# Split products for the first two weights of well-filled experts, branches on three engines, gate and scatter one group later

## The chip, the cores and the metric

The kernel runs on one core of one Trainium2 chip. The metric is the device time of one execution in microseconds (us). PE is the tensor engine, ACT the scalar engine (ScalarE), DVE the vector engine (VectorE), POOL is GpSimd, and SP issues the DMAs.

## The reference

The program is a decoder trunk of two layers over 256 tokens of width 1024. Each layer has a mixer (attention, convolution, a state-space part), a feed-forward part and a gated embedding. In the second layer the feed-forward part is a sum over eight experts of inner width 3584, of which each token uses its best two:

```python
def swiglu(x, w1, w3, w2):
    return (jax.nn.silu(x @ w1) * (x @ w3)) @ w2

def moe_swiglu(x, router, w1, w3, w2):
    logits = (x @ router).astype(jnp.float32)
    top_vals, top_idx = lax.top_k(logits, TOP_K)
    wts = jax.nn.softmax(top_vals, axis=-1)
    comb = jnp.einsum('blk,blke->ble', wts, jax.nn.one_hot(top_idx, N_EXPERTS, dtype=jnp.float32))
    for e in range(N_EXPERTS):
        y = y + comb[..., e:e + 1] * swiglu(x, w1[e], w3[e], w2[e])
```

All weights are f32, 44 MB an expert.

## The kernel before

**Loads.** `moe` goes through the experts one behind the other. `expert_loads` cuts an expert's weights into 42 loads of 1 MB (128 partitions by 2048 f32). The inner width is taken in four chunks (`CHUNKS`): three of 1024 columns, one of 512. A full chunk has four loads of w1 and four of w3, the last chunk two and two; 14 loads of w2 follow. `load` takes the next slot of a ring of 1 MB buffers (`self.ring`, `room`) and has SP issue the DMA. In the second layer the ring has 18 slots, built in `run`: buffers of earlier stages that are free by then, among them the four split buffers (`hl`) and one buffer of the residual stream (`xl`). A slot is written again when the products that read it are done. At the seventh expert (`e == OVF`) two slots go to the overflow path, which this input does not take, and the other 16 are all loaded ahead.

**Products.** `expert` emits groups of two loads (`GRP`) inside `either`, which is a branch on the expert's number of tokens `n`: over 64 (`SM`), plain f32 products with 128 columns of tokens as the weights of PE; up to 64, the two halves of a chunk run as products of 64 columns in two halves of PE. Both write the two accumulators `mgu` of w1, then of w3 (L1468); w2 writes `mo` (L1503). Only PE reads `n` and branches; the other engines have only unconditional jumps between the blocks. An expert's w1 and w3 make 14 groups, w2 seven. A plain f32 product shows in the trace as two records.

**Gate, turn, scatter.** Behind the last w3 group of a chunk ACT applies Silu to w1's accumulators (L1475) and DVE multiplies with w3's (L1476), half by half. What is put into the list `todo` is emitted behind the next group by `flush`: `turn`, which has PE transpose the gated values (`hT`, L1444) and ACT and DVE copy them into `ht` (L1449, L1447), and for the finished expert `scatter`, which multiplies its result with the slot matrix on PE and adds it to `y` on DVE (L1526). The result is first split into a high and a low part (`ot`, L313 on ACT and L314 on DVE). DVE also clears accumulators (L1432).

**Split products.** Elsewhere (the dense feed-forward, the last gate) a weight is split into `whl`: ACT copies it to the reduced-precision type f32r (L313), DVE subtracts that from the weight (L314), 1024 columns at a time in `parts`; `mm3` (L308 to L310) then makes three products: high by high, low tokens by high weight, high tokens by low weight.

A scheduler sets the order within each engine; each engine takes its instructions strictly in that order.

Of the kernel before, what the change touches and what calls it, by code (L numbers as in the profile page):

```python
# [7 lines left out]
F32 = mybir.dt.float32  # L8
F32R = mybir.dt.float32r
I32 = mybir.dt.int32  # L10
U32 = mybir.dt.uint32
AF = mybir.ActivationFunctionType
# [3 lines left out]
P = 128  # L16
D = 1024
S = 256
TT = S // P
KT = D // P  # L20
# [135 lines left out]
RBN = 2  # L156
OV = 2
HB = 4
GRP = 2
SM = 64  # L160
OVF = 6
# [31 lines left out]
class Trunk:  # L193
# [1042 lines left out]
    def moe(self, l, mp):  # L1236
        nc, a, sm = self.nc, self.a, self.sm
# [100 lines left out]
        for e in range(NE):  # L1338
            if e == OVF:

                self.flush()
                ov = self.over
                main = self.turned(ov[:2])
                self.ring, self.nload = main, 0
                self.pre = [self.load(*s) for s in self.expert_loads(j, e)[: len(main)]]
                self.ring, self.nload = [ov] * ov[2], 0
                pre, self.pre = self.pre, []
                self.overflow(j, mp, Da[:, e // 2 % 2], cint, th, tl, rank, sel, comb, y)
                self.ring, self.pre, self.nload = main + self.ring, pre, len(main)
                pair(e)  # L1350
            Dm = Da[:, e // 2 % 2]
            es = ts(e % 2)
            De = [Dm[:, tt, e % 2] for tt in range(TT)]
            D2 = mp.tile([P, TT, P], F32, tag="D2", name="D2")
            for tt in range(TT):
                nc.vector.tensor_scalar(D2[:, tt], slots, rank2[:, tt, e : e + 1], sel[:, tt, e : e + 1], op0=ALU.is_equal, op1=ALU.mult)
            ce = [comb[:, tt, e : e + 1] for tt in range(TT)]
            n = nc.tensor.value_load(cint[0:1, e + 1 : e + 2], min_val=0, max_val=S)
            ahead = (lambda: pair(e + 1)) if e % 2 and e + 1 not in (OVF, NE) else None
            last = e == NE - 1  # L1360
            self.expert(mp, self.expert_loads(j, e), n, self.xh[:, :, es], De, [D2[:, tt] for tt in range(TT)], ce, y, ahead, norm if last else None)
            if e == NE - 2:

                lnp = self.ln_params(l, 1, mp, "tl")
                more = mp.tile([P, 2, D], F32R, tag="th", name="more")
                bias = self.ple_bias(l, mp.tile([P, D], F32, tag="h2", name="gb"), more[:, 0])
# [34 lines left out]
                    yield  # L1401

    def flush(self):
        while self.todo:
            self.todo.pop(0)()

    def either(self, n, emit):

# [9 lines left out]
    def expert(self, mp, loads, n, xe, Dm, D2, comb, y, ahead=None, done=None):  # L1418

        nc = self.nc
        mm = nc.tensor.matmul
        loads = iter(loads)
        get = lambda: [self.pre.pop(0) if (s := next(loads)) and self.pre else self.load(*s) for _ in range(GRP)]
        rows = (slice(0, SM), slice(P - SM, P))

        def pair(name):
            acc = self.pair(name)
            if n is not None:  # L1430
                for h in range(2):
                    nc.vector.memset(acc[h][rows[1 - h]], 0.0)  # L1432
            return acc

        hts = []

        def turn(ci, hw, hbs):

            nb = hw // P
            ht = mp.tile([P, 2 * nb, P], F32, tag=f"h{ci}", name="ht", bufs=1)  # L1440
            for h in range(2):
                ps = self.tr("hT")
                for i in range(nb):
                    nc.tensor.transpose(ps[:, i * P : (i + 1) * P], hbs[h][:, i * P : (i + 1) * P], self.ident)  # L1444
                dst = ht[:, h * nb : (h + 1) * nb].rearrange("p k t -> p (k t)")
                if h:
                    nc.vector.tensor_copy(dst, ps[:, :hw])  # L1447
                else:
                    nc.scalar.activation(dst, ps[:, :hw], AF.Copy)  # L1449
                hts.extend((ht[:, h * nb + i], h) for i in range(nb))  # L1450

        DT = []
        for ci, (c0, cw) in enumerate(CHUNKS):
            hw, ku = cw // 2, 2048 // cw
            accs = []
            for wi in range(2):
                acc = pair("mgu")
                for u0 in range(0, KT // ku, GRP):
                    ws = get()

                    def emit(few):
                        for u, w in enumerate(ws):
                            for i in range(ku):
                                k = (u0 + u) * ku + i
                                for h in range(2):
                                    wk = w[:, i, h * hw : (h + 1) * hw]
                                    dst, x = (acc[h][rows[h], :hw], xe[:, k, 0:SM]) if few else (acc[h][:, :hw], xe[:, k])
                                    mm(dst, x, wk, start=k == 0, stop=k == KT - 1)  # L1468

                    self.either(n, emit)  # L1470
                accs.append(acc)
            hbs = []
            for h in range(2):
                hb = mp.tile([P, 512], F32, tag="hb", name="hb", bufs=2)
                nc.scalar.activation(hb[:, :hw], accs[0][h][:, :hw], AF.Silu)  # L1475
                nc.vector.tensor_mul(hb[:, :hw], hb[:, :hw], accs[1][h][:, :hw])  # L1476
                hbs.append(hb)
            self.todo.append(lambda ci=ci, hw=hw, hbs=hbs: turn(ci, hw, hbs))
            if ci == 0:

                def turn_slots():

                    t = mp.tile([P, 2, TT, P], F32R, tag="DT", name="DT", bufs=1)
                    ps = self.tr("DT")
                    for i, src in enumerate([v.bitcast(F32) for v in Dm] + D2):
                        nc.tensor.transpose(ps[:, i * P : (i + 1) * P], src, self.ident)
                    nc.scalar.activation(t.rearrange("p h t s -> p (h t s)"), ps, AF.Copy)
                    DT.append(t)

                self.todo.append(turn_slots)  # L1490
        acc = pair("mo")
        NK = D_FFE // P
        for g in range(0, NK // 2, GRP):
            ws = get()

            def emit(few):
                for u, w in enumerate(ws):
                    for i in range(2):
                        k = 2 * (g + u) + i
                        ht, hf = hts[k]  # L1500
                        for h in range(2):
                            dst, x = (acc[h][rows[h]], ht[:, rows[hf]]) if few else (acc[h], ht)
                            mm(dst, x, w[:, i, h * 512 : (h + 1) * 512], start=k == 0, stop=k == NK - 1)  # L1503

            self.either(n, emit)
            if g == GRP and ahead:
                ahead()
        ots = []
        for h in range(2):
            ot = mp.tile([P, 2, 512], F32R, tag=f"h{h}", name="ot", bufs=1)  # L1510
            self.split(ot[:, 0], ot[:, 1], acc[h])
            ots.append(ot)

        def scatter():
            normed = ()
            if done:
                self.ring, self.nload = self.turned((self.cp, "xl")), 0
                self.new_xT()
            for tt in range(TT):
                sc = self.pair("sc")  # L1520
                for h in range(2):
                    hs = slice(h * 512, (h + 1) * 512)
                    mm(sc[h], DT[0][:, h, tt], ots[h][:, 0], start=True, stop=False)
                    mm(sc[h], DT[0][:, h, tt], ots[h][:, 1], start=False, stop=True)
                    with self.after(*normed):
                        nc.vector.scalar_tensor_tensor(y[:, tt, hs], sc[h], comb[tt], y[:, tt, hs], op0=ALU.mult, op1=ALU.add)  # L1526
                if done:
                    normed = done(tt)[1:]

        if n is None or done:  # L1530
            scatter()
        else:
            self.todo.append(scatter)

    def overflow(self, j, mp, Dm, cint, th, tl, rank, sel, comb, y):

# [91 lines left out]
    def rest(self, l, ffn):  # L1628
        pool = lambda n: self.tc.tile_pool(name=f"{n}{l}", bufs=1)

        with self.open, pool("ra") as ra, pool("re") as re, pool("rd") as rd, pool("rb") as rb, pool("th") as th:
            if l % 2:
                self.ring = [(rb, "raw", RBN)] * RBN + [(self.st, "raw", RB)] * RB + [(self.xp, "pp", 1), (ra, "raw", 1)]
                self.ring += [(self.st, "hl", HB)] * HB + [(self.cp, "xl", 1)]
                self.ring += [(re, "raw", 2)] * 2
                self.nload = len(self.ring) - 2
                self.over = (rd, "raw", OV)
                self.ring += [self.over] * OV
# [52 lines left out]
```

## Time and profile before

| what | value |
|---|---|
| median of 3 runs | 1608.57 us (1608.24 to 1608.64) |
| the profiled execution, its own time | 1610.99 us |
| its span in the profile | 1608.8 us |
| mean granted clock of PE | 0.959 |
| PE busy | 1454.2 us, 90% of the span |
| DVE, ACT busy | 678.0 us (42%), 401.3 us (25%) |
| 16 DMA engines, q1 | 73.3% of the span, 437.42 MB |
| expert loads | 336 of 1024 KB |

The expert stage lies between about 620 and 1536 us of the span. A busy share is a mean over stages with different limits; the chain of waits (what ended last, followed back) and windows of single stretches tell which of them sets the time. Inside a bracket behind a row of a timeline stands the idle time of that engine just before the row and what ended it.

### The profile page before, as it was taken

How to read it: one execution, taken by the hardware profiler on the slowest of the kernel's cores; microseconds unless marked ns; L12 is line 12 of the kernel's file. 1: busy time of each engine (PE TensorE's matmuls, PEld its weight loads, DVE VectorE, ACT ScalarE, POOL GpSimd, SP SyncE). 2: the span in 40 equal slices, each digit the busy share in tenths (PEclk: the TensorE clock that was granted, in tenths of full speed). 3: DMA queues.
4: the chain of work that ended last, by engine and by line, in shares of the span. 5: the costliest groups of instructions: out<-in, count | busy, mean ns of one | idle time of the engine just before them, and what ended most of it. 6: DMA issues, size and time to landing. Idle time of an engine off the chain costs nothing. (4 is left out here: it accounts for less than half of the span.)

```text
span 1608.8 us, 16526 instructions
## 1 busy us (share of the span) xinstructions
PE 1454.2 (90%) x6318; PEld 832.5 (52%) x6319; DVE 678.0 (42%) x1105; ACT 401.3 (25%) x719; POOL 266.0 (17%) x205
## 2 busy tenths in 40 slices
PE   6776999999888699998899999999999998998776
PEld 6544788876675475432344643444644454342234
DVE  8989648646778955222121103121102102122137
ACT  6454555434466431100001001000000000000023
POOL 4855106612124511000000000000000000010012
PEclk9787999999998888999999999999999999999999
DMA  7431365553462049999999999999898878999971
GB/s 250 137 152 40 124 214 187 192 170 131 170 192 111 27 158 401 403 408 405 407 409 402 409 344 389 408 410 400 299 308 272 301 238 281 362 408 409 402 288 53
DMA packets 139625, 445.28 MB, mean 277 GB/s; under 512 B 7408, under 2 KB 19312, under 8 KB 138496
## 3 DMA queue, kind: packets, MB, share of 16 engines
q1 hardware_dynamic: 138496, 437.42, 73.3%
q0 software_dynamic: 1024, 6.38, 1.1%
q8 instruction: 76, 1.25, 0.3%
q14 instruction: 29, 0.24, 0.0%
HBM read 442.72 MB, written 1.05 MB: 276 GB/s over the span
## 5 line engine op out<-in xcount | busy, mean ns | idle before, releaser
L1468 PE MATMUL mgu<-wraw,xe 128*64 128x512 f32 (+3 forms) x2048 | 548.5, 542 | 25.4 <-DMA wraw<-in_moe_w_dram 17.3
L1468 PEld LDWEIGHTS mgu<-wraw,xe 128*64 128x64 f32 (+1 forms) x2048 | 238.3, 157 | 318.4 <-issue 246.9
L1503 PE MATMUL mo<-wraw,ht 128*64 128x512 f32 (+1 forms) x896 | 272.0, 595 | 12.4 <-DMA wraw<-in_moe_w_dram 12.4
L1503 PEld LDWEIGHTS mo<-wraw,ht 128*64 128x64 f32 (+1 forms) x896 | 101.0, 157 | 172.0 <-issue 143.1
L314 DVE TENSOR_TENSOR whl<-wraw,whl 128x1024 fp32r<-128x1024 f32 (+2 forms) x106 | 136.5, 1297 | 81.7 <-ACT whl L313 81.1
L313 ACT ACTIVATE whl<-wraw 128x1024 fp32r<-128x1024 f32 (+3 forms) x109 | 107.5, 994 | 138.3 <-PE fffn_w L310 44.6
L1476 DVE TENSOR_TENSOR hb<-hb,mgu 128x512 f32<-128x512 f32 (+1 forms) x64 | 37.9, 618 | 236.1 <-PE mgu L1468 235.7
L510 POOL DMA_DIRECT2D lnp<-in_lnp_dram x5 | 2.8, 566 | 772.6 <-ACT xe L1397 744.1
L1449 ACT ACTIVATE ht<-hT 128x512 f32<-128x512 f32 (+1 forms) x32 | 17.4, 544 | 393.4 <-PE hT L1444 378.0
L314 DVE TENSOR_TENSOR ot<-mo,ot 128x512 fp32r<-128x512 f32 x16 | 10.6, 688 | 243.1 <-ACT ot L313 243.1
L1432 DVE MEMSET mgu<- 64x512 f32 x128 | 62.1, 485 | 100.2 <-ACT hb L1475 84.1
L1447 DVE COPY ht<-hT 128x512 f32<-128x512 f32 (+1 forms) x32 | 20.0, 625 | 140.7 <-PE hT L1444 136.7
L310 PE MATMUL fffn_w<-whl,xh 128*128 128x512 f32 (+1 forms) x192 | 71.8, 374 | 0.0
L309 PE MATMUL fffn_w<-whl,xl 128*128 128x512 f32 (+1 forms) x192 | 71.7, 373 | 0.0
L308 PE MATMUL fffn_w<-whl,xh 128*128 128x512 f32 (+1 forms) x192 | 71.4, 372 | 0.0
L1475 ACT ACTIVATE hb<-mgu 128x512 f32<-128x512 f32 (+1 forms) x64 | 32.4, 543 | 152.1 <-PE mgu L1468 149.0
L313 ACT ACTIVATE ot<-mo 128x512 fp32r<-128x512 f32 x16 | 9.0, 596 | 239.6 <-PE mo L1503 239.6
L957 DVE SCALAR_TENSOR_TENSOR cy<-upad,pk,cy 128x256 f32<-128x256 f32 x60 | 56.6, 943 | 1.2
L308 PEld LDWEIGHTS fffn_w<-whl,xh 128*128 128x128 f32 x192 | 36.1, 188 | 6.7
L309 PEld LDWEIGHTS fffn_w<-whl,xl 128*128 128x128 f32 x192 | 36.1, 188 | 6.6
L310 PEld LDWEIGHTS fffn_w<-whl,xh 128*128 128x128 f32 x192 | 36.1, 188 | 6.2
L1444 PEld LDWEIGHTS hT<-sqr,hb 128*128 128x128 f32 x224 | 24.8, 140 | 24.7 <-issue 20.4
(371 smaller groups left out, 2147.0 us busy)
## 6 DMA issues: line engine op xcount, KB each, us to landing
wraw<-in_moe_w_dram SPq DMA_DIRECT2D x336, 1024.0 KB, 17.5
wraw<-in_ffn_w_dram SPq DMA_DIRECT2D x33, 1024.0 KB, 5.2
wraw<-in_cmp_w_dram SPq DMA_DIRECT2D x8, 1024.0 KB, 5.6
wraw<-in_w_out_dram SPq DMA_DIRECT2D x8, 1024.0 KB, 7.2
wraw<-in_ple_gate_w_dram SPq DMA_DIRECT2D x8, 1024.0 KB, 5.0
wraw<-in_w_in_dram SPq DMA_DIRECT2D x8, 792.0 KB, 5.9
wraw<-in_w_in_dram SPq DMA_DIRECT2D x8, 768.0 KB, 8.0
lnp<-in_lnp_dram POOLq DMA_DIRECT2D x5, 1024.0 KB, 5.2
```

The costliest lines, as they stand in the source:

```text
L308: mm(dst, xh, wh, start=start, stop=False)
L309: mm(dst, xl, wh, start=False, stop=False)
L310: return mm(dst, xh, wl, start=False, stop=stop)
L313: h = self.hi = self.nc.scalar.activation(dh, src, AF.Copy)
L314: return h, (low or self.nc.vector).tensor_tensor(dl, src, dh.bitcast(F32), op=ALU.subtract)
L957: nc.vector.scalar_tensor_tensor(y0, u(0, k), w(0, k), y0, op0=ALU.mult, op1=ALU.add)
L1432: nc.vector.memset(acc[h][rows[1 - h]], 0.0)
L1444: nc.tensor.transpose(ps[:, i * P : (i + 1) * P], hbs[h][:, i * P : (i + 1) * P], self.ident)
L1468: mm(dst, x, wk, start=k == 0, stop=k == KT - 1)
L1475: nc.scalar.activation(hb[:, :hw], accs[0][h][:, :hw], AF.Silu)
L1476: nc.vector.tensor_mul(hb[:, :hw], hb[:, :hw], accs[1][h][:, :hw])
L1503: mm(dst, x, w[:, i, h * 512 : (h + 1) * 512], start=k == 0, stop=k == NK - 1)
```

## The change

An expert with over 64 tokens takes w1 and w3 as split products: each load is split in two pieces of 1024 columns on ACT and DVE and multiplied by `mm3`. Therefore ACT and DVE read `n` too and branch in `either` (`BRANCH`). The gathered tokens `xe` are split once an expert into `xs`. The four `hl` buffers and `xl` now hold the split weights and the split tokens, and leave the ring, which keeps 13 slots. `gate` (Silu and product) and the scatter become entries of `todo`, and `flush` runs only the entries that were there when it began, so each entry that an entry adds comes one group later. w2 stays plain.

```diff
@@ moe @@
-            n = nc.tensor.value_load(cint[0:1, e + 1 : e + 2], min_val=0, max_val=S)
+            n = nc.values_load(cint[0:1, e + 1 : e + 2], engines=BRANCH, min_val=0, max_val=S)
@@ flush @@
-        while self.todo:
-            self.todo.pop(0)()
+        todo, self.todo = self.todo, []
+        for f in todo:
+            f()
@@ expert @@
+        xs = self.cp.tile([P, 2, KT, P], F32R, tag="xl", name="xs")
+        self.split(xs[:, 0], xs[:, 1], xe)
         hts = []
+
+        def gate(ci, hw, accs):
+            hbs = []
+            for h in range(2):
+                hb = mp.tile([P, 512], F32, tag="hb", name="hb", bufs=2)
+                nc.scalar.activation(hb[:, :hw], accs[0][h][:, :hw], AF.Silu)
+                nc.vector.tensor_mul(hb[:, :hw], hb[:, :hw], accs[1][h][:, :hw])
+                hbs.append(hb)
+            self.todo.append(lambda: turn(ci, hw, hbs))
...
                         for u, w in enumerate(ws):
-                            for i in range(ku):
+                            for i, wh, wl in [(i, w[:, i], None) for i in range(ku)] if few else self.parts(w, ku, cw):
                                 k = (u0 + u) * ku + i
                                 for h in range(2):
-                                    wk = w[:, i, h * hw : (h + 1) * hw]
-                                    dst, x = (acc[h][rows[h], :hw], xe[:, k, 0:SM]) if few else (acc[h][:, :hw], xe[:, k])
-                                    mm(dst, x, wk, start=k == 0, stop=k == KT - 1)
+                                    hs = slice(h * hw, (h + 1) * hw)
+                                    if few:
+                                        mm(acc[h][rows[h], :hw], xe[:, k, 0:SM], wh[:, hs], start=k == 0, stop=k == KT - 1)
+                                    else:
+                                        self.mm3(acc[h][:, :hw], xs[:, 0, k], xs[:, 1, k], wh[:, hs], wl[:, hs], k == 0, k == KT - 1)
...
-            self.todo.append(lambda ci=ci, hw=hw, hbs=hbs: turn(ci, hw, hbs))
+            self.todo.append(lambda ci=ci, hw=hw, accs=accs: gate(ci, hw, accs))
...
-        for h in range(2):
-            ot = mp.tile([P, 2, 512], F32R, tag=f"h{h}", name="ot", bufs=1)
-            self.split(ot[:, 0], ot[:, 1], acc[h])
-            ots.append(ot)
+
+        def result():
+            for h in range(2):
+                ot = mp.tile([P, 2, 512], F32R, tag=f"h{h}", name="ot", bufs=1)
+                self.split(ot[:, 0], ot[:, 1], acc[h])
+                ots.append(ot)
+            self.todo.append(scatter)
...
-        if n is None or done:
-            scatter()
-        else:
-            self.todo.append(scatter)
+        self.todo.append(result)
+        while self.todo and (n is None or done):
+            self.flush()
@@ run @@
-                self.ring += [(self.st, "hl", HB)] * HB + [(self.cp, "xl", 1)]
```

ACT in the second chunk of the third expert, an expert with over 64 tokens. In the order before, `mgu_6185` and `mgu_6186` are the accumulators of w1; nothing but jumps stands between these instructions:

```order
L1449 ACTIVATE ht_6210<-hT_6211 128x512
L1487 ACTIVATE DT_6223<-DT_6224 128x512
L1412 UNCONDITIONAL_BRANCH
L1475 ACTIVATE hb_6297<-mgu_6185 128x512
L1412 UNCONDITIONAL_BRANCH
L1475 ACTIVATE hb_6300<-mgu_6186 128x512
L1412 UNCONDITIONAL_BRANCH x2
L1449 ACTIVATE ht_6328<-hT_6329 128x512
```

The same place after; `mgu_7157` is the first half of w1's accumulators of this chunk, `wraw_7223` and `wraw_7225` are the loads of its second w1 group, `wraw_7289` is the first load of w3:

```order
L1465 ACTIVATE ht_7272<-hT_7273 128x512
L1416 COMPARE_AND_BRANCH
L314 ACTIVATE whl_7228<-wraw_7223 128x1024
L314 ACTIVATE whl_7237<-wraw_7223 128x1024
L314 ACTIVATE whl_7246<-wraw_7225 128x1024
L314 ACTIVATE whl_7255<-wraw_7225 128x1024
L1416 UNCONDITIONAL_BRANCH x2
L1448 ACTIVATE hb_7440<-mgu_7157 128x512
L1416 COMPARE_AND_BRANCH
L314 ACTIVATE whl_7294<-wraw_7289 128x1024
```

The `ht` copy of the chunk before now stands ahead of the splits of the second w1 group, and the Silu of this chunk ahead of the splits of the first w3 group.

DVE at the end of the same chunk, before; `mgu_6251` and `mgu_6252` are the accumulators of w3:

```order
L1412 UNCONDITIONAL_BRANCH
L1476 TENSOR_TENSOR hb_6297<-hb_6297,mgu_6251 128x512
L1412 UNCONDITIONAL_BRANCH
L1476 TENSOR_TENSOR hb_6300<-hb_6300,mgu_6252 128x512
L1432 MEMSET mgu_6414 64x512
L1432 MEMSET mgu_6415 64x512
L1447 COPY ht_6328<-hT_6335 128x512
L1412 UNCONDITIONAL_BRANCH x2
```

And after; `mgu_7285` and `mgu_7286` are the accumulators of w3, `wraw_7340` is the last load of w3, `wraw_7391` and `wraw_7393` are the first w1 group of the next chunk:

```order
L315 TENSOR_TENSOR whl_7370<-wraw_7340,whl_7370 128x1024
L1416 UNCONDITIONAL_BRANCH x2
L1449 TENSOR_TENSOR hb_7440<-hb_7440,mgu_7285 128x512
L1416 COMPARE_AND_BRANCH
L315 TENSOR_TENSOR whl_7396<-wraw_7391,whl_7396 128x1024
L315 TENSOR_TENSOR whl_7405<-wraw_7391,whl_7405 128x1024
L315 TENSOR_TENSOR whl_7414<-wraw_7393,whl_7414 128x1024
L315 TENSOR_TENSOR whl_7423<-wraw_7393,whl_7423 128x1024
L1416 UNCONDITIONAL_BRANCH x2
L1449 TENSOR_TENSOR hb_7443<-hb_7443,mgu_7286 128x512
```

The product of the first half stands between the last w3 splits and the next chunk's first splits, that of the second half and, behind two memsets, the `ht` copy ahead of the next chunk's second group.

## Rows read from the trace of the kernel before

**Rows 1.** Chain that ended last: shares of the span; start, duration, what.

```profile
by line: DMA wraw<-in_moe_w_dram 4.4%; PE mgu L1468 4.2%; PE mo L1503 1.5%; DMA wraw<-in_ple_gate_w_dram 1.1%; PE xe L1393 0.4%; PE pg L310 0.4%; PE pg L308 0.4%; issue 0.4%; PE pg L309 0.3%; DVE glo L553 0.3%; DVE x L531 0.3%; DVE x L532 0
...
1501.53 34.18 DMA wraw<-in_moe_w_dram x2
1535.77 18.09 DMA wraw<-in_ple_gate_w_dram
```

**Rows 2.** Windows: length, busy of PE, PEld, DVE, ACT, POOL, clock, DMA share, GB/s.

```profile
720.00:740.00 20.00, 15.70 (x72) 5.19 (x74) 4.68 (x11) 2.28 (x4) 0.00 (x0) 1.00 1.03 409
...
1300.00:1320.00 20.00, 19.85 (x52) 9.04 (x51) 1.27 (x3) 0.38 (x1) 0.00 (x0) 1.00 0.66 212
1340.00:1360.00 20.00, 15.26 (x46) 8.48 (x45) 6.59 (x12) 1.20 (x2) 0.00 (x0) 0.89 0.68 221
```

**Rows 3.** Page, DMA issues: count, size, median us from issue to landing.

```profile
wraw<-in_moe_w_dram SPq DMA_DIRECT2D x336, 1024.0 KB, 17.5
wraw<-in_ffn_w_dram SPq DMA_DIRECT2D x33, 1024.0 KB, 5.2
```

**Rows 4.** Timeline of PE, third expert: start, duration, instructions [idle before, what ended it].

```profile
808.91 7.10 PE L1468 MATMUL mgu<-wraw,xe 128*128 128x512 f32 x16 [0.70 <-ACT ot L313]
...
817.69 27.63 PE L1468 MATMUL mgu<-wraw,xe 128*128 128x512 f32 x64
845.16 1.04 PE L1444 MATMUL hT<-sqr,hb 128*128 128x128 f32 x8
...
903.66 7.07 PE L1468 MATMUL mgu<-wraw,xe 128*128 128x256 f32 x32
910.91 0.41 PE L1444 MATMUL hT<-sqr,hb 128*128 128x128 f32 x2 [0.17 <-DVE hb L1476]
...
959.54 0.65 PE L1468 MATMUL mgu<-wraw,xe 128*64 128x512 f32 x2
```

**Rows 5.** Groups by line and form: busy, mean ns | idle before.

```profile
L1468 PE MATMUL mgu<-wraw,xe 128*128 128x512 f32 x576 | 249.8, 593 | 2.0 <-ACT ot L313 0.7 <-ACT hb L1475 0.7 <-DVE mgu L1432 0.6
```

**Rows 6.** Chain that ended last, start of the seventh expert.

```profile
1363.29 20.75 PE mgu L1468 x96
```

**Rows 7.** Timelines of ACT, DVE and PE, split operands and gathers.

```profile
244.88 1.23 DVE L314 TENSOR_TENSOR whl<-wraw,whl 128x1024 fp32r<-128x1024 f32 x1 [1.52 <-ACT whl L313]
...
276.15 1.06 ACT L313 ACTIVATE whl<-wraw 128x1024 fp32r<-128x1024 f32 x1 [1.69 <-PE fffn_w L310]
278.89 1.06 ACT L313 ACTIVATE whl<-wraw 128x1024 fp32r<-128x1024 f32 x1 [1.69 <-PE fffn_w L310]
...
621.92 0.28 PE L1393 MATMUL xe<-Dm,th 128*128 128x256 f32 x1
622.04 0.28 PE L1393 MATMUL xe<-Dm,tl 128*128 128x256 f32 x1
...
622.48 9.76 PE L1468 MATMUL mgu<-wraw,xe 128*64 128x512 f32 x44
```

**Rows 8.** Timelines of ACT and DVE, third expert.

```profile
818.07 1.99 DVE L1526 SCALAR_TENSOR_TENSOR x<-sc,comb,x 128x512 f32<-128x512 f32 x3
...
853.15 0.60 ACT L1475 ACTIVATE hb<-mgu 128x512 f32<-128x512 f32 x1 [5.41 <-PE mgu L1468]
867.74 0.69 DVE L1476 TENSOR_TENSOR hb<-hb,mgu 128x512 f32<-128x512 f32 x1 [0.17 <-PE mgu L1468]
875.10 0.60 ACT L1449 ACTIVATE ht<-hT 128x512 f32<-128x512 f32 x1 [20.50 <-PE hT L1444]
...
958.84 0.60 ACT L313 ACTIVATE ot<-mo 128x512 fp32r<-128x512 f32 x1 [47.10 <-PE mo L1503]
```

**Rows 9.** Timeline of PE, last gate.

```profile
1558.18 0.80 PE L310 MATMUL pp<-whl 128*128 128x512 f32 x1 [1.80 <-POOL whl L314]
...
1560.06 0.63 PE L308 MATMUL pp<-whl 128*128 128x512 f32 x1
1560.48 0.63 PE L309 MATMUL pp<-whl 128*128 128x512 f32 x1
```

More of the change, by code (lines that the diff above doesn't have):

```diff
@@ L158 @@
 HB = 4
+BRANCH = (mybir.EngineType.PE, mybir.EngineType.Activation, mybir.EngineType.DVE)
 GRP = 2
@@ L1339, in moe @@
             if e == OVF:
-                self.flush()
+                while self.todo:
+                    self.flush()
                 ov = self.over
@@ L1462, in emit @@
                         for u, w in enumerate(ws):
-                            for i in range(ku):
+                            for i, wh, wl in [(i, w[:, i], None) for i in range(ku)] if few else self.parts(w, ku, cw):
                                 k = (u0 + u) * ku + i
                                 for h in range(2):
-                                    wk = w[:, i, h * hw : (h + 1) * hw]
-                                    dst, x = (acc[h][rows[h], :hw], xe[:, k, 0:SM]) if few else (acc[h][:, :hw], xe[:, k])
-                                    mm(dst, x, wk, start=k == 0, stop=k == KT - 1)
+                                    hs = slice(h * hw, (h + 1) * hw)
[3 more added lines that the diff above has]
+                                        self.mm3(acc[h][:, :hw], xs[:, 0, k], xs[:, 1, k], wh[:, hs], wl[:, hs], k == 0, k == KT - 1)
                     self.either(n, emit)
                 accs.append(acc)
-            hbs = []
-            for h in range(2):
[L1474 to L1477, printed above, removed]
-            self.todo.append(lambda ci=ci, hw=hw, hbs=hbs: turn(ci, hw, hbs))
+            self.todo.append(lambda ci=ci, hw=hw, accs=accs: gate(ci, hw, accs))
             if ci == 0:
@@ L1508, in expert @@
         ots = []
-        for h in range(2):
-            ot = mp.tile([P, 2, 512], F32R, tag=f"h{h}", name="ot", bufs=1)
-            self.split(ot[:, 0], ot[:, 1], acc[h])
-            ots.append(ot)
+        def result():
[4 more added lines that the diff above has]
+            self.todo.append(scatter)
         def scatter():
@@ L1528, in scatter @@
                     normed = done(tt)[1:]
-        if n is None or done:
-            scatter()
-        else:
-            self.todo.append(scatter)
+            self.turn += 2
+        self.todo.append(result)
+        while self.todo and (n is None or done):
+            self.flush()
     def overflow(self, j, mp, Dm, cint, th, tl, rank, sel, comb, y):
```

## The prediction

> **What bounds the kernel now.** I read the chain that ended last first, then the windows, then single rows of the third expert. The chain ends on transfers: the last two expert weights land at 1535.77, the two loads of the last layer end the rest, and expert loads are the largest single share of it [rows 1]. The windows show two regimes in the expert stage. In an expert with few tokens the DMA engines are full (408 to 409 GB/s) and PE is busy 15.70 of 20 us; in an expert with many, PE is busy 19.85 of 20 and the transfers drop to half [rows 2]. So there are two prices. One load is 1.0486 MB [rows 3], at 408.5 GB/s 2.57 us; 42 loads, one expert, 107.8 us. PE needs 20.75 for 96 records of an expert with few tokens [rows 6], 3.46 for a group of 16, 1.73 a load: it waits for the loads. The third expert has many tokens: from 808.91 to 959.54 PE takes 150.6 [rows 4], 43 more than its loads do. There are 576 records of its first form [rows 5], 192 an expert, so three experts are of this kind: third, fifth and sixth. What sets the end is a ledger. While PE lags, the loads run ahead until the ring is full; what they are ahead by when the seventh expert starts (1363.29 [rows 6]) is all that counts, since the last two experts are bound by transfers. Proof: 16 loads are ahead there (18 slots less two for the overflow), 84 − 16 = 68 remain, 68 × 2.57 = 174.7, which gives 1538 against 1535.8 in the chain. So the time is (start of the seventh expert) + 2.57 × (loads still to land) + a tail that the change leaves alone. The profiled execution (1610.99) lies 2.4 above the median; I add differences to the median, 1608.57.
>
> **What is removed.** Plain products: 64 records last from 817.69 to 845.16, 0.429 each, 192 make 82.4; the half-wide ones take 7.07 per 32 [rows 4], less the tail of the last about 0.215 each, 64 make 13.9. Sum 96.3 an expert. Added are 288 split products. In the dense feed-forward, twelve of them lie between two splits of the same kind, 2.74 [rows 7], so 0.229 each: 65.9. The 96 half-wide ones start 0.12 apart (two gathers of 256 columns [rows 7]): 11.5. Sum 77.4, which is **−18.9 an expert** if PE never waits.
>
> **What PE waits for.** A group is now four pieces; each needs one copy on ScalarE (1.06) and one subtraction on VectorE (1.23 [rows 7]), and feeds PE for 6 × 0.229 = 1.37. So in the steady state PE is last and VectorE's 56 pieces (69) fit under the 77.4. But the order of the two engines, as shown in the change's section, puts instructions that wait for PE's newest product between the splits of one group and the next. Silu of w1's first half stands ahead of the copies of w3's first group, though the change speaks of a gate one group later; the product of Silu stands behind w3's last group and ahead of the next chunk's first; the ht copies stand ahead of the next chunk's second group. Queued behind each are the next four splits, and for those PE waits. Before, the same Silu also stood idle 5.41 for PE, and the ht copy 20.50 [rows 8], and nobody was behind them. Only PE branched then. PE can start a piece with its two products that need only the copy (0.46), so each stop costs:
> Silu: 0.60 [rows 8] + 1.06 + 1.23 − 0.46, less 0.45 since the half that it reads is done three products (0.69) ahead and a hop comes off that, = 2.0. Product of Silu: 0.69 [rows 8] + 1.23 − 0.46 − 0.45 = 1.0. Copies of ht, behind transposes that last 1.04 [rows 4]: 0.60 + 1.06 + 1.23 − 0.46, less about 0.32 for the first half, = 2.1. A full chunk 5.1, two of those 10.2. The first chunk has no ht copy, but the previous expert's result (0.60 [rows 8] + 1.06 + 1.23 − 0.46 = 2.4) and its scatter on VectorE (four of 0.66, as three last 1.99 [rows 8], + 1.23 − 0.46 = 3.4) and the Silu stop: 7.8. The last chunk is one group for each weight: 1.0, and ht with Silu in one stop 2.7, and half of a row of transposes 0.5: 4.2. **Sum +22.3 an expert.** Bounds: nothing if ScalarE and VectorE get to these instructions after PE is done (their order says no) and 30, if each hop costs 0.2 more and the two halves do not overlap. I take the worked sum.
>
> **Branches.** The third expert has 14 groups with new branches on two engines. Before, no compare-and-branch stands on them; the nearest row is VectorE's gate, 0.17 after PE's last product with an unconditional jump between [rows 8]. 14 × 0.17 = **+2.4**; bounds 0 (hidden under the stops) and 4.8 (both engines). In experts with few tokens the splits are jumped over and PE waits for loads anyway: nothing, until that cover, 0.84 a load, is used up. The split of the gathered tokens (copy and subtraction once an expert) lies beside w2 of the expert before. W2 and its products are left alone.
>
> Together −18.9 + 22.3 + 2.4 = +5.8 an expert, three of them **+17.4** on the start of the seventh.
>
> **The smaller ring.** The four split buffers and one token buffer leave the ring: 13 slots, not 18. Three places. At the start, PE's first expert product is at 622.48 [rows 7]; by then 13 loads have landed and the queue never stood still. Now the 14th, with all later loads behind it on SP, waits for the first group (3.46) and then for a load's way of 5.2 [rows 3] less its own 2.57: +6.1. In the third expert the loads run up to the end of the ring; the fourth, where PE gains 0.84 × 42 = 35 on them, uses up nearly all that it then has (11 × 2.57 = 28 to 33): about +1, bounds 0 and 8. At the seventh 11 loads are ahead, not 16: 5 × 2.57 = +12.8, hidden by nothing. **Sum +20**, bounds 12 (the start hidden by the gathers) and 27.
>
> Forecast: 1608.57 + 17.4 + 20 = **1646**; by the bounds, as far as they are not (A) and (B) below, 1616 (stops 15, ring 12) to 1676 (stops 30, ring 27).
>
> **Rivals.** (A) The gate does what its words say: PE finds each piece ready. Then each many expert saves 18.9 and only the ring is paid: 1608.57 − 56.7 + 20 = **1572**, 1565 to 1602 with some of the stops. For it: VectorE needs 69 of 77 us and the four buffers are a group ahead. Against: the order, in which splits queue behind PE's newest product. The change turns faster when the stops come to less than 10 an expert (−18.9 + 9.8 + 2.4, three times, pays the ring's 20). 0.12.
> (B) The stops are half as long, 11: hops and halves overlap better, or the scatter is hidden. −18.9 + 11 + 2.4 = −5.5, three −16.5, + 20: **1612**, 1602 to 1622. This is the case of no change. 0.13.
> (C) Slower by TensorE's clock. Products that follow a wait for a split late in the kernel start 0.42 apart [rows 9] where 0.229 stands above, and the window 1340 to 1360, with short waits, was granted 0.89 of 2.4 GHz [rows 2]: some of it at 1.2 GHz. Against it: 15.70 busy of 20 with the gaps of the loads kept 1.00 [rows 2]. If one group of 24 products in each of 3.5 chunks runs at half clock, 24 × 0.20 × 3.5 × 3 = +50: **1696**. It decides from waits that the many experts don't have today. 0.09.
> The Trainium skill, "TensorE: Matmul & The Clock Gate", section "A second HAM failure mode: psum-queue depth-cycling", tells of a kernel whose PE was idle for short times between groups of products so often that its clock went back and forth between the two levels, at a cost in throughput. By that rule (C) would be the likeliest, at 1696; the trace agrees at 1558 and not at 720, and I leave it a rival.
> (D) The change does not do what it says: no expert is sent into the split path. Then only the ring is paid, 1608.57 + 20 = **1629**. Against it: the condition (over 64 tokens) is the one that sends three experts to the 128-wide products today [rows 5]. 0.02.
>
> **How the numbers follow.** Forecast 0.64, (A) 0.12, (B) 0.13, (C) 0.09, (D) 0.02. What a measurement of this kernel can tell from no change is about 0.2%, 3.2 us. Faster: (A) and the low end of (B), 0.14. Same: the part of (B) about 1608, 0.06. Slower: the rest of (B), the forecast, (C) and (D), 0.80. The range takes in the forecast's bounds and (B): 1602 to 1680; (A) and (C) stay out.
>
> **What would show it.** After: in the third expert a full chunk takes about as long as before (some 29 us for 27.5 of products before) though its products add to 22; PE idles 1 to 2.5 at three of four groups, ended by ScalarE's or VectorE's split; the w1 and w3 stage lasts 105 to 108 where it was 102; the granted clock stays at 1.00 there. A gap of about 6 in the transfers near 620. The seventh expert starts some 25 later, and its two experts take 13 more. I am wrong if PE runs through group after group in the third expert with no idle time (A), if the stops are there but near 0.8 each (B), or if the products there show 0.42 (C).

## The result and the profile after

The changed kernel takes 1668.55 us (median of 4 runs, 1666.12 to 1674.16), the kernel before 1608.4 beside it: 1.0379 times as long, 95% interval 1.0351 to 1.0407. The time lies inside the range of 1602 to 1680, 22.5 above the forecast of 1646. The profiled execution of after took 1666.99, its span 1665.2, 56.4 more than the span before.

The stage in which the third expert multiplies w1 and w3 shows what happened. A stop below is idle time of PE in front of a product. PE's timeline from the first product of w3 in the first chunk to the second chunk's first products (start, duration, instruction, idle time before it and what ended that):

```profile
838.23 0.50 PE L309 MATMUL mgu<-whl,xs 128*128 128x512 f32 x1 [1.40 <-ACT whl L314]
838.57 0.40 PE L310 MATMUL mgu<-whl,xs 128*128 128x512 f32 x1
839.49 0.79 PE L311 MATMUL mgu<-whl,xs 128*128 128x512 f32 x1 [0.52 <-DVE whl L315]
840.08 0.63 PE L309 MATMUL mgu<-whl,xs 128*128 128x512 f32 x1
840.50 0.63 PE L310 MATMUL mgu<-whl,xs 128*128 128x512 f32 x1
...
843.00 0.40 PE L310 MATMUL mgu<-whl,xs 128*128 128x512 f32 x1
843.24 0.39 PE L311 MATMUL mgu<-whl,xs 128*128 128x512 f32 x1
...
848.84 0.50 PE L311 MATMUL mgu<-whl,xs 128*128 128x512 f32 x1 [0.54 <-DVE whl L315]
849.18 0.40 PE L309 MATMUL mgu<-whl,xs 128*128 128x512 f32 x1
...
852.85 0.40 PE L310 MATMUL mgu<-whl,xs 128*128 128x512 f32 x1
854.47 0.51 PE L311 MATMUL mgu<-whl,xs 128*128 128x512 f32 x1 [1.22 <-DVE whl L315]
```

These are the stops of one pass: 1.40 + 0.52 at the first w3 group (Silu was ahead of its copies), 0.54 at the second piece of the second group, 1.22 at the next chunk's first (the gate's product was ahead of its subtractions). Two more things are to be seen. A product that follows a stop takes 0.34 to the next one (848.84 to 849.18), not 0.23. And from 840.08 the products start 0.42 apart, from 843.00 again 0.23. Windows of the two stretches (length, busy of PE, PEld, DVE, ACT, POOL, granted clock, DMA share, GB/s) show a granted clock of 0.50, the lower of PE's two levels, and then 1.00:

```profile
839.60:842.80 3.20, 3.20 (x8) 2.52 (x9) 3.20 (x3) 2.96 (x4) 0.00 (x0) 0.50 1.01 406
844.00:848.00 4.00, 4.00 (x19) 3.05 (x17) 1.71 (x3) 1.53 (x2) 0.00 (x0) 1.00 1.03 410
```

It does not follow every such stop. In the fifth expert the same two stops leave the products 0.23 apart:

```profile
1092.75 0.50 PE L309 MATMUL mgu<-whl,xs 128*128 128x512 f32 x1 [1.41 <-ACT whl L314]
...
1094.01 0.50 PE L311 MATMUL mgu<-whl,xs 128*128 128x512 f32 x1 [0.53 <-DVE whl L315]
1094.35 0.39 PE L309 MATMUL mgu<-whl,xs 128*128 128x512 f32 x1
1094.58 0.39 PE L310 MATMUL mgu<-whl,xs 128*128 128x512 f32 x1
```

ACT and DVE in the second chunk of the third expert:

```profile
869.83 0.60 ACT L1448 ACTIVATE hb<-mgu 128x512 f32<-128x512 f32 x1 [5.17 <-PE mgu L310]
870.32 3.89 ACT L314 ACTIVATE whl<-wraw 128x1024 fp32r<-128x1024 f32 x4
...
860.71 0.69 DVE L1463 COPY ht<-hT 128x512 f32<-128x512 f32 x1 [0.98 <-PE hT L1460]
861.85 4.63 DVE L315 TENSOR_TENSOR whl<-wraw,whl 128x1024 fp32r<-128x1024 f32 x4 [0.45 <-ACT whl L314]
```

ACT stands 5.17 for PE's product, then does Silu, and only then the four copies of the next group: the same Silu that waited 5.41 before [rows 8], but now with the pieces that PE needs next queued behind it. All stops of the three experts together, from the groups by line and form (busy, mean ns, idle before by cause):

```profile
L311 PE MATMUL mgu<-whl,xs 128*128 128x512 f32 x288 | 124.9, 434 | 26.5 <-DVE whl L315 26.2
L309 PE MATMUL mgu<-whl,xs 128*128 128x512 f32 x288 | 123.1, 427 | 29.2 <-ACT whl L314 29.2
L309 PE MATMUL mgu<-whl,xs 128*128 128x256 f32 x96 | 27.4, 288 | 5.2 <-ACT whl L314 5.2
L311 PE MATMUL mgu<-whl,xs 128*128 128x256 f32 x96 | 27.2, 294 | 5.2 <-DVE whl L315 5.2
```

26.5 + 29.2 + 5.2 + 5.2 = 66.1, **22.0 an expert**, where before the plain products had 2.0 for all three [rows 5]. The three stages as windows:

```profile
817.40:936.20 118.80, 97.61 (x419) 75.67 (x420) 83.72 (x91) 60.48 (x70) 0.00 (x0) 0.91 0.85 325
1071.50:1184.70 113.20, 92.15 (x419) 70.80 (x420) 83.73 (x91) 60.26 (x69) 0.00 (x0) 0.97 0.90 344
1234.40:1351.60 117.20, 95.96 (x419) 73.75 (x420) 82.68 (x89) 59.40 (x68) 0.00 (x0) 0.93 0.68 244
```

Before they lasted 102.2, 103.2 and 103.0 at a clock of 1.00. The transfers, around the first expert's start, before and then after:

```profile
615.00:627.00 12.00, 11.82 (x58) 8.74 (x60) 8.13 (x37) 3.97 (x5) 4.53 (x2) 0.73 1.02 409
```

```profile
615.00:627.00 12.00, 9.28 (x41) 6.10 (x39) 6.99 (x24) 2.25 (x3) 0.64 (x1) 0.75 0.13 31
```

The 13 slots are full soon after 615, and nearly nothing moves until PE has ended its first group. Last, PE's first products on the last expert weights to land, before and after; the first row of after is the first product of the seventh expert:

```profile
1546.09 1.94 PE L1503 MATMUL mo<-wraw,ht 128*64 128x512 f32 x8 [0.66 <-DMA wraw<-in_moe_w_dram]
```

```profile
1415.06 10.52 PE L1484 MATMUL mgu<-wraw,xe 128*64 128x512 f32 x48
...
1606.47 1.94 PE L1515 MATMUL mo<-wraw,ht 128*64 128x512 f32 x8 [0.66 <-DMA wraw<-in_moe_w_dram]
```

So the 56.4 of the span divide like this, by the times at which the same work starts:

| stretch | before | after | more |
|---|---|---|---|
| span's start to the third expert's first product | 808.91 | 817.46 | 8.6 |
| w1 and w3, third, fifth, sixth expert | 102.2, 103.2, 103.0 | 118.7, 113.1, 117.1 | 40.5 |
| rest up to the seventh expert's first product (1363.2, then 1415.06) | | | 2.8 |
| from there to the last expert weights | 182.9 | 191.4 | 8.5 |
| from there to the end | 62.7 | 58.7 | −4.0 |

### The profile page after: what moved, and what is told of

It reads as the page before. It is cut to its first block, busy times and chain, and to the rows that moved or that the text cites. A ratio compares the mean times of both kernels' runs of the same rounds, so it can differ in the third digit from the quotient of the medians.

```text
span 1665.2 us, 18717 instructions
## 1 busy us (share of the span) xinstructions
PE 1433.8 (86%) x6702; PEld 893.2 (54%) x6703; DVE 878.1 (53%) x1281; ACT 572.5 (34%) x895; POOL 265.6 (16%) x205
## 3 DMA queue, kind: packets, MB, share of 16 engines
q0 software_dynamic: 1024, 6.38, 1.0%
## 5 line engine op out<-in xcount | busy, mean ns | idle before, releaser
L315 DVE TENSOR_TENSOR whl<-wraw,whl 128x1024 fp32r<-128x1024 f32 (+2 forms) x274 | 331.2, 1246 | 220.4 <-ACT whl L314 219.7
L314 ACT ACTIVATE whl<-wraw 128x1024 fp32r<-128x1024 f32 (+2 forms) x277 | 272.3, 1027 | 190.8 <-PE mgu L311 50.3
L1484 PE MATMUL mgu<-wraw,xe 128*64 128x512 f32 (+1 forms) x1280 | 256.8, 547 | 34.3 <-DMA wraw<-in_moe_w_dram 24.9
L1484 PEld LDWEIGHTS mgu<-wraw,xe 128*64 128x64 f32 x1280 | 92.3, 138 | 189.5 <-issue 142.9
L309 PE MATMUL mgu<-whl,xs 128*128 128x512 f32 (+1 forms) x384 | 150.5, 393 | 34.4 <-ACT whl L314 34.4
L311 PE MATMUL mgu<-whl,xs 128*128 128x512 f32 (+1 forms) x384 | 152.1, 399 | 31.8 <-DVE whl L315 31.5
L310 PE MATMUL mgu<-whl,xs 128*128 128x512 f32 (+1 forms) x384 | 146.6, 383 | 0.0
L311 PEld LDWEIGHTS mgu<-whl,xs 128*128 128x128 f32 x384 | 76.9, 201 | 62.8 <-DVE whl L315 50.8
L309 PEld LDWEIGHTS mgu<-whl,xs 128*128 128x128 f32 x384 | 77.0, 201 | 56.2 <-ACT whl L314 45.3
L1465 ACT ACTIVATE ht<-hT 128x512 f32<-128x512 f32 (+1 forms) x32 | 17.4, 543 | 228.3 <-PE hT L1460 228.2
L310 PEld LDWEIGHTS mgu<-whl,xs 128*128 128x128 f32 x384 | 77.4, 201 | 12.9
```

Of the source, the lines that this page charges most:

```text
L309: mm(dst, xh, wh, start=start, stop=False)
L310: mm(dst, xl, wh, start=False, stop=False)
L311: return mm(dst, xh, wl, start=False, stop=stop)
L314: h = self.hi = self.nc.scalar.activation(dh, src, AF.Copy)
L315: return h, (low or self.nc.vector).tensor_tensor(dl, src, dh.bitcast(F32), op=ALU.subtract)
L1484: mm(acc[h][rows[h], :hw], xe[:, k, 0:SM], wh[:, hs], start=k == 0, stop=k == KT - 1)
```

## The experiments

The theory after this look: the stops come from what the splits queue behind on ACT and DVE (22 an expert, some 66 us in all), they pull the clock down (20 more), the ring costs 13, the branches nothing. The rivals: the split work itself, above all DVE's 84 us of 118, is the limit; the branches cost; the clock falls for another reason.

**The ring alone.** The kernel before with

```diff
-                self.ring += [(self.st, "hl", HB)] * HB + [(self.cp, "xl", 1)]
```

> The kernel before with nothing changed but the ring: the four split buffers and the token buffer leave it, 13 slots, not 18. If the ring's part of the loss is what the trace of after shows (first w1 product of the third expert 8.6 later, last expert load 8.5 later counted from the seventh expert's start, tail 4 shorter), the time is 1608.4 + 13 = 1621, up to 1628 if the third to sixth experts also lose lead. If the ring costs nothing, and all of the 60 lies in the experts with many tokens: 1607 to 1611.

1621.19 us, 1.008 times the kernel before (1.006 to 1.0101): +12.3. The gap in the transfers is there, with no split in the program:

```profile
615.00:627.00 12.00, 12.00 (x59) 6.26 (x61) 5.71 (x24) 2.48 (x3) 0.04 (x1) 0.91 0.51 172
627.00:640.00 13.00, 13.00 (x64) 5.33 (x62) 3.23 (x6) 1.56 (x3) 0.00 (x0) 1.00 0.66 230
```

and the third expert starts at 817.11, as in after. The stages of the three experts last 102.25, 103.2 and 103.0, untouched. The ring's price is shown: 12 of the 60.

**The branches alone.** The kernel before with `values_load(..., engines=BRANCH, ...)`, no splits.

> The kernel before with nothing changed but that ScalarE and VectorE read the count and branch too; no splits, ring of 18. My theory: they branch beside PE's work and nobody waits, 1608 to 1611. Rival: the branches cost what I put down for them, 2.4 in each of three experts, 1616, or more if all eight pay, 1625.

1607.64 us, ratio 0.9993 (0.9983 to 1.0002). Two more engines that branch cost nothing that can be measured in all eight experts together, in a program where these engines have no splits to do.

**The order, forced.** After, with everything that `flush` emits tied behind the branch of the group just emitted, on each engine, and the ht copies one group behind their transposes:

```diff
-        self.flush()
+            self.cond = many.cond_inst
+        with self.behind():
+            self.flush()
...
+            def copies():
...
+            self.todo.append(copies)
```

> After, with the order of the gate forced: Silu and its product are queued behind the next group's branch, transposes with them, the ht copies one group later again, so that no split stands behind an instruction that waits for PE's newest product. Same products, same ring, same branches. My theory (the waits are this order, 22 an expert, and the clock falls because of them): waits for splits under 8 an expert, w1 and w3 stage of the third expert from 118.8 to 90 to 98, granted clock there 0.98 or more, time 1585 to 1605. Rival (VectorE's 84 busy of such a stage, or the split chain itself, is the limit): stage 108 or more, time 1640 or more.

1647.84 us, 1.0233 times before (1.0215 to 1.0251): 21 of the 60 come back, the stages are 111, 109 and 109 long. Both sides missed: the stage is above the first theory's range and the time below the rival's. ACT's waits went as they should (from 34.4 in all to 7.5), but DVE's grew from 31.7 to 44.8. ACT's timeline shows what was left:

```profile
842.37 1.06 ACT L325 ACTIVATE whl<-wraw 128x1024 fp32r<-128x1024 f32 x1 [5.85 <-PE mgu L322]
847.68 3.90 ACT L325 ACTIVATE whl<-wraw 128x1024 fp32r<-128x1024 f32 x4 [4.26 <-PE mgu L322]
854.09 2.96 ACT L325 ACTIVATE whl<-wraw 128x1024 fp32r<-128x1024 f32 x3 [2.50 <-PE mgu L322]
```

One piece, then a wait for PE's last product of the group before, then the other three with the next group's first. I read this as the four split buffers: a group is four pieces, and the copies into the second to fourth buffer start only when PE has ended the group before, so ACT is one piece ahead and not a group. Why they do not start piece by piece is not shown. So each group pays for one more subtraction (0.53), and behind the gate's two products and four memsets on DVE it pays 1.95.

**PE kept busy during the stops.** After, with six products of a zero weight tile ahead of seven groups an expert:

```diff
...
+                        stop = (not wi and u0) or (wi and not u0)
+                        for q in range(6 if stop and not few else 0):
+                            mm(acc[q % 2][:, :hw], zero, xs[:, 0, 0 : hw // P].rearrange("p k t -> p (k t)"), start=u0 == 0, stop=u0 == 0)
```

> After, with six products of a zero weight tile ahead of the first split product in the seven groups an expert where PE waits for ScalarE's split; they add zero or are overwritten. The splits come no sooner, so the waits for them stay in place, but PE works during most of them. If TensorE's clock falls because PE stands still there (third expert 0.91 granted, 54 products at 0.43): granted clock 0.97 or more in the three stages, stage of the third 108 to 114, time 1645 to 1660. If the clock does not hang on these waits: clock as in after, stage the same or 2 to 4 longer, 1668 to 1680.

1659.5 us, 1.0316 times before (1.0297 to 1.0334), nine less than after although PE does 126 products more. The windows of its three stages:

```profile
816.40:927.30 110.90, 99.06 (x461) 76.75 (x462) 83.89 (x92) 60.27 (x69) 0.00 (x0) 0.98 0.90 349
1063.00:1177.20 114.20, 101.88 (x461) 79.25 (x462) 83.88 (x92) 60.27 (x69) 0.00 (x0) 0.96 0.89 339
1226.90:1338.30 111.40, 99.11 (x461) 76.83 (x462) 82.68 (x89) 59.42 (x68) 0.00 (x0) 0.98 0.71 256
```

The clock rose from 0.91 to 0.98 and from 0.93 to 0.98 in two stages and fell from 0.97 to 0.96 in one, against my expectation of 0.97 in all three. Counted in the timelines, the split products that start 0.42 apart (0.21 the half-wide ones) lost some 9, 4 and 7 in after, 20 together, and 10 here. That idle time of PE at these stops brings the lower level, and with it half of the 20, is shown for the sum and for two stages of three; DVE's stops, which the filler does not cover, are left in all of them. Which stop brings it is not shown.

**Shorter pieces.** After, each piece split in two halves of 512 columns:

```diff
-            self.split(hi, lo, flat, low)
+            if halves:
+                for q in range(2):
+                    hs = slice(q * n // 2, (q + 1) * n // 2)
+                    self.split(hi[:, hs], lo[:, hs], flat[:, hs], low)
+            else:
+                self.split(hi, lo, flat, low)
```

> After, with each piece of 1024 columns split in two instructions of 512 on either engine; same buffers, order, products. If the waits are one copy and one subtraction behind a late instruction, each becomes shorter by 0.46 on ScalarE and 0.54 on VectorE: eight stops of an expert by 1.0, six by 0.5, less some 0.15 a piece where VectorE is late: waits of an expert from 22.5 to 12 to 16, time 1640 to 1655. If the split work as such is the limit (more instructions, more fixed cost): waits 22 or more, time 1668 to 1690.

1627.06 us, 1.0105 times before (1.0087 to 1.0124), better than I thought: 41 of the 60 come back. The stops fell from 66 to 39.5 (13.2 an expert):

```profile
L316 PE MATMUL mgu<-whl,xs 128*128 128x512 f32 x288 | 119.5, 415 | 12.7 <-DVE whl L320 12.7
L314 PE MATMUL mgu<-whl,xs 128*128 128x512 f32 x288 | 117.6, 408 | 20.2 <-ACT whl L319 20.2
```

(the half-wide products have 2.7 and 3.9). The stages are 102.2, 102.7 and 103.6 long, as long as before; DVE is busy longer in them, 87 instead of 84, in stages that are 10 to 16 shorter. DVE's throughput was not the limit; the time from a late instruction to the first finished piece was. Since the stages are as long as before, the 18 that are left lie outside them: the ring's 12, and 6 that no run places.

**Without the delay.** After, but Silu, its product and the result's split emitted right behind their group, as before the change.

> After without its third part: Silu, its product and the result's split are emitted right behind their group again, only transposes and the scatter one group later. My theory: the scheduler had put the gate there anyway, so nothing changes: 1660 to 1675, waits for splits 20 to 25 an expert. Rival (the delayed gate does hide something): 1690 or more.

1681.08 us, 1.0445 times before (1.0427 to 1.0462), 12.5 slower than after: my expectation missed. The stages are 121.4, 116.8 and 121.5, 10.7 more in all; the stops are 68 instead of 66, and the clock is lower:

```profile
821.40:942.80 121.40, 99.76 (x423) 77.06 (x423) 84.36 (x93) 60.56 (x69) 0.00 (x0) 0.90 0.83 318
1078.40:1195.30 116.90, 94.68 (x423) 72.99 (x424) 84.35 (x93) 60.55 (x70) 0.00 (x0) 0.94 0.87 330
```

So the third part of the change is worth something, though the gate stands at the same places in the steady chunks. Some 6 of the 10.7 in the stages are again the clock (products at 0.42 lose 25 to 26, in after 20), by one profile of each.

**Groups of one load.** The forced order with `GRP = 1`, so that four buffers are two groups.

> The forced order with groups of one load instead of two. In the trace of the forced order ScalarE's second piece of every group waits until PE has ended the group before, since the four split buffers are exactly one group; with groups of one load (two pieces) the next group's pieces find two free buffers while PE works. If this lookahead is what still stops PE there (0.53 at each group and the long stops behind the gate): waits for splits under 8 an expert, stage of the third expert 92 to 100, time 1590 to 1615. If VectorE's own work is the limit, or twice as many branches cost what the waits give back: stage 106 or more, time 1640 or more.

1660.52 us, ratio 1.0308 (1.0283 to 1.0332). The time tells nothing on the buffers, since with smaller groups the scheduler put the third expert's first products between the second expert's w2 groups, and PE then waited for a load that is queued behind all of w2's:

```profile
823.03 0.80 PE L320 MATMUL mgu<-whl,xs 128*128 128x512 f32 x1 [18.71 <-ACT whl L325]
```

The sixth expert, where PE did not wait for a load, does tell something. Its full-wide products stop 5.8 for DVE, where they stopped 12.3 in the forced order (first row: the forced order, second: groups of one load):

```profile
L322 PE MATMUL mgu<-whl,xs 128*128 128x512 f32 x96 | 41.0, 427 | 12.3 <-DVE whl L326 12.3
L322 PE MATMUL mgu<-whl,xs 128*128 128x512 f32 x96 | 38.7, 403 | 5.8 <-DVE whl L326 5.8
```

That supports the reading of the buffers. It does not prove it, as some of this expert's products stand between w2 groups of the expert before; a run with more split buffers was not made.

**Order and halves, and what else DVE does.** Both edits together, and then ("best") the clearing of the accumulators' unused halves moved to where it is needed:

```diff
-            if n is not None:
-                for h in range(2):
-                    nc.vector.memset(acc[h][rows[1 - h]], 0.0)
...
+                        if few and u0 == 0:
+                            clear(acc)
```

> The forced order and the pieces split in halves together. If the two act on different parts of the waits (which instruction the splits queue behind, and how long one piece takes from there), the stage of an expert with many tokens falls below both (109 to 111 forced, 102 to 104 with halves) to 94 to 99, waits of an expert under 10, and the time from 1627 to 1600 to 1614, that is about the kernel before. If VectorE is the limit in both, 101 or more and 1622 to 1632.

> The same with the clearing of the accumulators' unused halves moved into the branch of experts with few tokens, the only ones that need it: 20 memsets of 0.66 less on VectorE in an expert with many. If VectorE is what the last waits hang on (in the forced order the long ones stand behind two products of the gate and four memsets, 1.95 each): stage 88 to 94, time 1588 to 1603, faster than the kernel before. If not: as forced_halves within 3.

1618.8 us for the two (1.0058 times before, 1.0041 to 1.0075), stages of 99 to 100 and waits of 11.6 an expert, all three worse than I expected; 9.2 to 9.6 of the remaining waits in each are for DVE. The third edit took those: **1589.95 us, 0.9871 times the kernel before** (0.985 to 0.9892). The stages of this version:

```profile
822.00:909.10 87.10, 84.00 (x421) 69.69 (x422) 78.22 (x129) 65.86 (x125) 0.00 (x0) 1.00 1.03 406
1046.40:1132.50 86.10, 83.30 (x422) 69.80 (x421) 76.39 (x126) 64.22 (x122) 0.00 (x0) 1.00 1.03 405
1180.60:1267.10 86.50, 83.70 (x422) 69.88 (x421) 73.62 (x121) 62.19 (x118) 0.00 (x0) 1.00 0.91 335
```

15 to 17 less than before a stage, and the clock at 1.00 throughout. The stops left are 4.2 and 5.1 for all three:

```profile
L325 PE MATMUL mgu<-whl,xs 128*128 128x512 f32 x288 | 114.6, 398 | 4.2 <-ACT whl L330 4.2
L327 PE MATMUL mgu<-whl,xs 128*128 128x512 f32 x288 | 114.0, 396 | 5.1 <-DVE whl L331 5.1
```

The stages gain 48.7 together, the time only 19. The ring takes its 12, and more is lost in the experts with few tokens, where the clearing now stands in front of PE's products. There PE's products of w1 and w3 wait 39.6 instead of 29.8, 8.2 of it for the clearing and 11.5 with no cause that the profile shows; how much of that sets the time is not shown (first row: after, second: this version):

```profile
L1484 PE MATMUL mgu<-wraw,xe 128*64 128x512 f32 x960 | 219.8, 602 | 29.8 <-DMA wraw<-in_moe_w_dram 22.1 <-ACTq L1416 5.5 <-DVE mgu L1436 1.4
L1512 PE MATMUL mgu<-wraw,xe 128*64 128x512 f32 x960 | 228.0, 614 | 39.6 <-DMA wraw<-in_moe_w_dram 19.3 <-issue 11.5 <-DVE mgu L1456 8.2
```

Which of the three edits carries it, by leaving one out:

> After with the halved pieces and the clearing moved into the branch of experts with few tokens, but without the forced order: which of the three edits carries the fastest version. If the order is what the splits wait for, the stops behind Silu and the ht copies stay (waits 10 to 13 an expert, stage 98 to 102, time 1610 to 1622). If it was the clearing alone: stage 88 to 92, 1592 to 1600.

> After with the forced order and the clearing moved, with whole pieces. By the same theory the 0.53 at the second piece of each group stays, since four buffers are one group: eight to ten of them, and the long waits behind the gate go: waits 7 to 11 an expert, stage 92 to 100, time 1602 to 1620. If the pieces' size does not matter then: stage 86 to 89, 1588 to 1594.

| version | stages of the three experts | stops in all | time |
|---|---|---|---|
| after | 118.7, 113.1, 117.1 | 66 | 1668.6 |
| forced order | 111.1, 109.0, 109.4 | 53 | 1647.8 |
| halves | 102.2, 102.7, 103.6 | 40 | 1627.1 |
| order and halves | 99.6, 99.6, 98.9 | 35 | 1618.8 |
| halves and clearing, no order | 96.5, 96.0, 96.5 | 31 | 1625.7 |
| order and clearing, whole pieces | 95.9, 96.7, 95.5 | 28 | 1616.5 |
| all three | 87.1, 86.1, 86.5 | 9 | 1590.0 |

Neither the order nor the halves do it alone, nor do any two of the three edits; the clearing alone was not run. Without the order ACT's waits stay (20.1 in the full chunks), with whole pieces DVE's (19.3 behind the first two products of a piece), both as expected. The time without the order came out 3.7 above my range, although its stages are shorter than I had put them. There the fourth expert, which has few tokens, gives some of it back, since PE now waits for the clearing inside its branch, a wait that before was beside the loads:

```profile
1001.45 4.32 PE L1491 MATMUL mgu<-wraw,xe 128*64 128x512 f32 x16 [1.55 <-issue]
```

## Why the prediction held, and where it was off

The time lies inside the range, but by luck. The upper end of the range was made of stops of 30 and a ring of 27. The stops came out at 22 and the ring at 13, and the clock, which the range left out, filled the room. By the prediction's own signs its mechanism was incomplete: it named 0.42 between products as the sign of being wrong by (C), and that is there. It put the stage at 105 to 108 at a clock of 1.00, and 113 to 119 at 0.91 to 0.97 were measured; the seventh expert was to start 25 later and started 52 later.

**What bounds the kernel.** The two regimes and the ledger (start of the seventh expert, loads still to land, a tail) held, and so did its count: 16 loads have landed when the seventh expert starts, two more are under way, and 68 remain. But 1535.77 is not where the last expert weights land. That is 1546, 182.7 behind the start instead of 174.7, because the transfers pause behind the start (271 GB/s from 1370 to 1380). That the sum met the chain was luck.

**What is removed and added.** −18.9 an expert was right: with 3 us of stops an expert the fastest version's stages are 15 to 17 shorter than before.

**The stops.** 22.3 was forecast, 22.8, 22.5 and 22.0 were measured. Singly: Silu 2.0 against 1.92, the product of Silu 1.0 against 1.22, the copies of ht 2.1 against 1.79 (1.26 + 0.53). Two errors nearly cancelled: the 0.53 at each second w3 group, 1.6 an expert, which I had not seen, and 0.2 to 0.4 too much in each chunk. I took the four buffers for a group of lead; the rows of ACT in the forced order read as one piece. The order alone does not give rival (A), the gate as its words say (1647.8, not 1572).

**The branches.** The term of 2.4 an expert was wrong in what it named, the lone branches cost nothing; about as much is lost at another place, the 0.11 that the first product behind each of some 22 stops takes longer.

**The clock.** This is the step that failed. I set it at nothing and kept it as rival (C) at +50; it took 20 in the three stages, by products at 0.42. The row on which the rival stood [rows 9] was the right one. The one that spoke against it [rows 2] was another case: there PE waits some 0.6 at a time for loads, and 1.58 once, at a clock of 1.00; here the stops are 0.3 to 2.1. Their length alone does not decide it, as 1.41 and 0.53 in the fifth expert left the clock at its higher level; what does is open. The Trainium skill, "TensorE: Matmul & The Clock Gate", section "A second HAM failure mode: psum-queue depth-cycling", says that a kernel with short idle times between its groups goes back and forth between the two levels and pays in throughput. The trace agrees in kind: about 50, 20 and 40 of 384 products at the lower level in the three experts, and 3 to 6 where the stops are gone.

**The ring.** +20 was forecast, 13 measured (12.3 alone on the kernel before). The start cost 8.6, not 6.1: after, the 13th load lands at 617.4, PE's first expert product comes only at 621.58, and the 14th lands at 630.4. This figure hangs on the profiles compared. With the lone branches and 18 slots the third expert starts at 804.76, 4.2 earlier than in the profile of before; against that one the start costs 12.4 with the ring alone and 12.7 after. From the seventh expert to the last expert weights after takes 8.5 more, not 12.8, since 13 loads have landed there and not the 11 of the prediction: three fewer than before, 3 × 2.57 = 7.7. The pause of the transfers is there in both. The tail was not left alone, it gave 4.0 back: before, SP has issued the last loads of the last gate only at 1558.5, while after all four are issued before the last expert weights land. That this is the cause is not shown: with groups of one load these loads are as early, and the tail is 62.8.

```profile
1535.77 22.76 SPq L249 DMA_DIRECT2D wraw<-in_ple_gate_w_dram  x3
```

```profile
1595.06 8.70 SPq L250 DMA_DIRECT2D wraw<-in_ple_gate_w_dram  x4
```

Together: 17.4 + 20 = 37.4 was the forecast; 40.5 for the experts (of it 20 the clock), 13.1 for the ring and 2.8 elsewhere make the 56.4 of the span. The 60 between the medians is more, as the profiled execution of before lies 2.4 above its median and that of after 1.6 below.

## What to carry to other kernels

When work for the busiest engine is put on engines that also run its epilogue, read each engine's order, not its busy time: an instruction that waits for the busiest engine's newest result turns everything queued behind it into a stall there. Price each such place as the time from that result to the first finished piece. Halving the pieces gave most back alone (41 of 60 us, the order 21); with what need not stand there moved away as well, the three edits together made the kernel 1.3% faster than before, while the order alone, the halves alone and every two left it slower. A ring that gives up slots costs their loads where the transfers are the limit, less whatever wait is there already.

## What was not expected of the hardware

A product that follows a stop of 0.5 to 1.7 us takes 0.34 to the next where 0.23 is usual, at the higher clock level. Three engines instead of one that compare and branch 168 times in a program cost nothing that ten runs can tell (1607.6 against 1608.9). Stops of 22 us in a stage, none over 2.2, cost 4 to 9 us more by the clock, at a mean granted clock of 0.91 to 0.97. The four runs of after spread over 8 us, and the two longest of them have the lowest clocks; those of the kernel before spread over 3 to 5 us in the larger series.
